# MLP's first product: raw x1 for twelve tiles, normed x1 for fifty-two, and the order of the transposes of x1

## The chip, the cores and the metric

The kernel runs on one core of a Trainium2 chip. The metric is the device time of one execution in microseconds (us); lower is better. TensorE (PE) multiplies, VectorE (DVE), ScalarE (ACT) and GpSimd (POOL) work on elements, and SyncE (SP) issues nearly all DMAs. Each engine works through its own instructions in order.

## The reference

One layer of a transformer with two recurrent branches, in float32, for 256 tokens of width D = 2048. The change touches what stands behind the branches:

```
x = x + g1 * ((gate_a * (ya @ up_a) + gate_b * (yb @ up_b)) @ out_w)      # called x1 here
h = x1 * rsqrt(mean(x1^2) + eps) * norm2_w * (1 + sc2) + sh2
x = x1 + g2 * (square(relu(h @ mlp_w1)) @ mlp_w2)                         # mlp_w1: 2048 x 8192
return rms_norm(x, final_norm_w)
```

## The kernel before

**Products in three parts.** A float32 operand is split into a high part (rounded copy in the fp32r type, on ACT) and a low part (the difference, on DVE). A product of two operands is three matmuls, high x high, high x low and low x high, added in one accumulator (`mm3`, `tokmm`).

**Weights** come in granules of 512 KB (`wgran`): SP issues the load into a `raw` buffer, then ACT copies the high part of each half of 512 columns (L235) and DVE subtracts (L236), both with the highest priority of the planner that lays out each engine's order. A pair of buffers (`hi`, `lo`) holds one half. There are three pairs (pool `stream`); from tile 6 of mix on (`RD`) four more come to them (`wide`, `NH2`), seven in all, and two more `raw` buffers to the three.

**Stages around the change.** *Mix*: 16 tiles, each one granule and 24 matmuls of 256 columns. *out_w*: four column blocks of 512; a block is eight granules of two k each (`tokmm`), 12 matmuls of 512 columns for a granule, with the weights as the moving operand; then `resid` adds the block to x (L1449, L1450: two steps on DVE for each half of the tokens). Right behind each block, its four 128-column pieces of x1 are turned by TensorE (L1477, eight transposes), scaled by norm2_w * (1 + sc2) on ACT (L1481) and split (L253, L254) into `xT[k]`, for k = 0 to 15.

*First product of the MLP* (w1), 64 tiles in two halves of 32: each tile is two granules and 16 x 3 matmuls of 258 columns. x1 is not normed: 256 columns are the scaled x1, and two more hold the shift sh2 (and a second one that is not used), so that h @ w1 comes out as rs * (x1s @ w1) + sh2 @ w1. The eviction multiplies by the row of rs (`rs_bc`, L1516), adds the shift's column inside the ReLU (L1515, L1517), squares (L1518) and splits the result into `uu[f]`. rs itself is made ahead of the first tile: `rstd` (sum on DVE, then a logarithm and an exponential on ACT, for which it loads tables, L1458, L1459), turned into a row by two matmuls (L1488). *Second product* (w2): after each half, `tokmm` over its 32 tiles, four blocks of 512 columns, 768 matmuls.

**Beside them**: `gate2` computes the gate g2 in 32 steps, each a load of 512 KB (L1410, SP) and two multiply-adds on DVE (L1416, L1418); one step stands ahead of each of the first 32 tiles in the code. The final norm's weight `fn` is loaded ahead of the first tile. Two accumulators of 512 columns alternate for `dacc`, four for `pm`. The planner lets an instruction go ahead of its place in the code when its engine would be free and its operands are there.

## Time and profile before

| | us |
|---|---|
| median of three runs | 2324.24 |
| lowest and highest of them | 2314.77 and 2326.75 |
| the profiled execution | 2329.58 |
| its span in the profile | 2327.8 |
| TensorE busy in the span | 2223.4 (96%) |
| DVE busy | 1579.1 (68%) |
| ACT busy | 1352.0 (58%) |

The profile shows one execution. "Busy" counts the time in which at least one instruction is recorded on an engine; records of matmuls overlap, as an end lies behind the next start, so the cost of a matmul in a row of them is read from start to start. Idle time in brackets is time in which nothing was recorded on the engine just ahead of the instruction, with what released it. Weight loads of TensorE have a row of their own (PEld) and lie beside the matmuls.

### The profile page before, as it was taken

The page shows a single profiled execution, that of the slowest core. Times are in us where ns is not written, and L with a number is a line of the kernel's source. Part 1 is how long each engine was busy: PE and PEld are TensorE (multiplying, and loading weights), DVE is VectorE, ACT ScalarE, POOL GpSimd, SP SyncE. Part 2 cuts the span into 40 slices and gives each one's busy share as a digit, 9 for nine tenths or more (in the row PEclk, how much of TensorE's full clock was granted, in tenths as well). Part 3 has the DMA queues.
Part 4 walks back from the last instruction along what each step waited for, and adds up shares of the span by engine and source line. Part 5 has one row for each costly group of instructions (what it writes and reads, how often), then busy time and mean ns, then how long its engine had stood idle before and what let it go on. Part 6 is the DMA issues. An engine that isn't in the chain of part 4 may idle for free.

```text
span 2327.8 us, 45179 instructions
## 1 busy us (share of the span) xinstructions
PE 2223.4 (96%) x16886; PEld 1809.3 (78%) x16886; DVE 1579.1 (68%) x3590; ACT 1352.0 (58%) x3003; POOL 159.1 (7%) x343
## 2 busy tenths in 40 slices
PE   5989999999999999999999999999999999999997
PEld 2566676767677776778888888879999888999886
DVE  2366875858686867678577766876887555666554
ACT  3244758575758575766666666555555444555543
POOL 0000021111111121111000000000000000000000
PEclk9998999999999999999999989999999999999999
DMA  9953333423333333457576455875776665555663
GB/s 369 330 177 129 103 111 106 141 89 123 109 128 116 123 118 108 138 187 245 191 228 223 159 151 162 304 256 181 258 266 217 191 194 195 182 182 182 193 195 128
DMA packets 184659, 418.20 MB, mean 180 GB/s; under 512 B 15412, under 2 KB 37364, under 8 KB 183416
## 3 DMA queue, kind: packets, MB, share of 16 engines
q1 hardware_dynamic: 183864, 414.28, 54.3%
q8 instruction: 132, 2.16, 0.4%
q10 hardware_dynamic: 576, 1.05, 0.1%
q14 instruction: 87, 0.71, 0.1%
HBM read 399.76 MB, written 15.51 MB: 178 GB/s over the span
## 4 chain that ended last, share of the span: by engine, by line
PE 73%; ACT 8%; DVE 6%; DMA 3%; issue 2%; DVEq 0%; ACTq 0%; SPq 0%
PE dacc L248 14%; PE dacc L249 13%; PE dacc L250 13%; PE dacc L1438 3%; PE dacc L1439 3%; PE dacc L1437 3%; PE pm L1437 3%; PE pm L1438 3%; PE pm L1439 3%; PE vacc L305 2%; DMA raw<-in_mod_w_dram 2%; ACT hi L235 1%; DVE lo L236 1%; PE cb L887 1%; PE pg L757 1%
## 5 line engine op out<-in xcount | busy, mean ns | idle before, releaser
L236 DVE TENSOR_TENSOR lo<-raw,hi 128x512 fp32r<-128x512 f32 (+1 forms) x1032 | 692.6, 677 | 439.0 <-ACT hi L235 264.1
L235 ACT CAST hi<-raw 128x512 fp32r<-128x512 f32 (+1 forms) x1032 | 624.5, 610 | 609.0 <-PE dacc L249 311.2
L248 PE MATMUL dacc<-hh,hi 128*128 128x256 f32 (+1 forms) x1648 | 567.1, 344 | 15.8 <-DVE sg L453 5.7
L250 PE MATMUL dacc<-hh,lo 128*128 128x256 f32 (+1 forms) x1648 | 534.6, 324 | 0.6 <-DVE lo L236 0.6
L249 PE MATMUL dacc<-hl,hi 128*128 128x256 f32 (+1 forms) x1648 | 533.7, 324 | 0.6 <-DVE hl L254 0.6
L248 PEld LDWEIGHTS dacc<-hh,hi 128*128 128x128 f32 x1648 | 317.6, 193 | 86.0 <-issue 42.6
L250 PEld LDWEIGHTS dacc<-hh,lo 128*128 128x128 f32 x1648 | 318.5, 193 | 24.4 <-issue 2.6
L249 PEld LDWEIGHTS dacc<-hl,hi 128*128 128x128 f32 x1648 | 318.9, 194 | 21.8 <-issue 3.2
L248 PE MATMUL dacc<-ah,hi 128*128 128x258 f32 x1024 | 291.9, 285 | 1.3 <-ACT ah L253 1.1
L249 PE MATMUL dacc<-al,hi 128*128 128x258 f32 x1024 | 291.1, 284 | 0.0
L250 PE MATMUL dacc<-ah,lo 128*128 128x258 f32 x1024 | 290.5, 284 | 0.0
L248 PEld LDWEIGHTS dacc<-ah,hi 128*128 128x128 f32 x1024 | 195.3, 191 | 2.8 <-ACT ah L253 1.3
L249 PEld LDWEIGHTS dacc<-al,hi 128*128 128x128 f32 x1024 | 195.1, 191 | 1.1 <-issue 1.0
L250 PEld LDWEIGHTS dacc<-ah,lo 128*128 128x128 f32 x1024 | 195.1, 191 | 0.0
L176 POOL TENSOR_SCALAR sp<-vu,pc 64x64 f32<-64x64 f32 x224 | 128.7, 574 | 432.0 <-DVE vu L176 379.8
L1438 PE MATMUL dacc<-hi,hl 128*128 128x512 f32 x320 | 125.4, 392 | 0.0
L1437 PE MATMUL dacc<-hi,hh 128*128 128x512 f32 x320 | 124.9, 390 | 0.3 <-ACT hh L253 0.3
L1439 PE MATMUL dacc<-lo,hh 128*128 128x512 f32 x320 | 125.1, 391 | 0.0
L1438 PE MATMUL pm<-hi,hl 128*128 128x512 f32 x320 | 124.8, 390 | 0.0
L1437 PE MATMUL pm<-hi,hh 128*128 128x512 f32 x320 | 124.8, 390 | 0.0
L1439 PE MATMUL pm<-lo,hh 128*128 128x512 f32 x320 | 124.7, 390 | 0.0
L494 DVE TENSOR_TENSOR ltmp<-X,Lt 128x126 f32<-128x126 f32 (+22 forms) x372 | 93.7, 252 | 8.1 <-DMA X<-in_eye_dram 0.8
(414 smaller groups left out, 3238.1 us busy)
## 6 DMA issues: line engine op xcount, KB each, us to landing
raw<-in_w_dram SPq DMA_DIRECT2D x256, 512.0 KB
raw<-in_mod_w_dram SPq DMA_DIRECT2D x96, 512.0 KB
graw<-in_mod_w_dram SPq DMA_DIRECT2D x96, 512.0 KB
raw<-in_w_gdn_dram SPq DMA_DIRECT2D x64, 512.0 KB
raw<-in_w_pg_dram SPq DMA_DIRECT2D x64, 512.0 KB
raw<-in_w_rkv_dram SPq DMA_DIRECT2D x40, 512.0 KB
raw<-in_out_w_dram SPq DMA_DIRECT2D x32, 512.0 KB
raw<-in_upa_dram SPq DMA_DIRECT2D x16, 512.0 KB
```

The lines of the kernel that those rows point to most:

```text
L176: return getattr(self.eng, name)(*a, **k)
L235: S.copy(out=hi[:, :F], in_=x)
L236: V.tensor_tensor(out=lo[:, :F], in0=x, in1=hi[:, :F].bitcast(F32), op=ALU.subtract)
L248: P.matmul(out=o, lhsT=wh, rhs=ah, start=first, stop=False)
L249: P.matmul(out=o, lhsT=wh, rhs=al, start=False, stop=False)
L250: P.matmul(out=o, lhsT=wl, rhs=ah, start=False, stop=last)
L305: P.matmul(out=pm[32 * g:32 * g + 32, :], lhsT=sc_st[:, 2 * k:2 * k + 32], rhs=raws[g // 2][:, g % 2 * 512:g % 2 * 512 + 512], start=(q == ...
L494: V.tensor_tensor(out=tv, in0=X[:, 0:n, j:j + 1].to_broadcast([128, n, 31 - j]), in1=Lt[:, j:j + 1, j + 1:32].to_broadcast([128, n, 31 - j ...
L757: P.matmul(out=q[:, c], lhsT=bkh(h, 4 + c), rhs=eb[r, h, c], start=True, stop=True)
L1437: P.matmul(out=pss[i], lhsT=ah[:, tsl], rhs=wh, start=first, stop=False)
L1438: P.matmul(out=pss[i], lhsT=al[:, tsl], rhs=wh, start=False, stop=False)
L1439: P.matmul(out=pss[i], lhsT=ah[:, tsl], rhs=wl, start=False, stop=last)
```

## The change

- The first product has two forms. The first `F0` = 12 tiles are as before. In the other 52 tiles x1 is normed and shifted already: `xN[k]` holds its high and low parts side by side, 256 columns each. One matmul of 512 columns multiplies the high weights with both, and one of 256 columns adds low weights x high part to the first half of the accumulator (`mm2`). The eviction adds the two halves, and takes ReLU and square in one step.
- `normed(k)` makes `xN[k]` from `xT[k]` during tiles 1 to 11: three steps on DVE and one on ACT for each k.
- High and low parts of an activation now lie in one tile (`hT`, `xT`, `xN`), so that one operand covers both. `xT` is four tiles `x0` to `x3`.
- Room: `xN` is new, and the four extra pairs of weight halves are gone. From tile 13 of w1 on, the space of `xT` (`x1` to `x3`) serves three more granules; of four granules three lie there and one in the `stream` pairs. `fn` goes into `x0`, loaded after the third block of the first w2 stage.
- `turned(n)`, the transposes and splits of block n, runs two granules into block n + 1 (the last one in the middle of the first tile of w1). `rstd` and its row come in the middle of the second tile, and the first tile is evicted after that. In the plain tiles the square moves from DVE to ACT.
- `gate2` steps once per two tiles from tile 12 on in the first half, then at every second granule of w2.

```diff
-NH2 = 4
-    nsplit, wide = 0, None
+    ngran, wide = 0, None
 
     def parts():
-        nonlocal nsplit
-        nsplit += 1
-        if not wide or nsplit % (3 + NH2) < 3:
-            return [stream.tile([128, 512], F32R, tag=t, name=t) for t in ("hi", "lo")]
-        return [wide.tile([128, 512], F32R, tag=t + "2", name=t, bufs=NH2) for t in ("hi", "lo")]
+        nonlocal ngran
+        ngran += 1
+        if not wide or ngran % 4 == 0:
+            return [[stream.tile([128, 512], F32R, tag=t, name=t) for t in ("hi", "lo")] for _ in range(2)]
+        w = wide.tile([128, 2, 2, 512], F32R, tag=f"x{ngran % 4}", name="w")
+        return [(w[:, i, 0, :], w[:, i, 1, :]) for i in range(2)]
         F = K // 2 * w
-        r = []
+        r = parts()
         for i in range(2):
-            hi, lo = parts()
+            hi, lo = r[i]
...
-    def mm3(o, wh, wl, ah, al, first, last):
-        P.matmul(out=o, lhsT=wh, rhs=ah, start=first, stop=False)
-        P.matmul(out=o, lhsT=wh, rhs=al, start=False, stop=False)
-        P.matmul(out=o, lhsT=wl, rhs=ah, start=False, stop=last)
-
-    def split(hi, lo, src):
-        S.copy(out=hi, in_=src)
-        V.tensor_tensor(out=lo, in0=src, in1=hi.bitcast(F32), op=ALU.subtract)
+    def mm3(o, wh, wl, a, first, last):
+
+        P.matmul(out=o, lhsT=wh, rhs=a[:, 0, :], start=first, stop=False)
+        P.matmul(out=o, lhsT=wh, rhs=a[:, 1, :], start=False, stop=False)
+        P.matmul(out=o, lhsT=wl, rhs=a[:, 0, :], start=False, stop=last)
+
+    def mm2(ps, wh, wl, a, first, last):
+
+        P.matmul(out=ps.rearrange("p (a n) -> p a n", a=2), lhsT=wh, rhs=a, start=first, stop=False, skip_group_check=True)
+        P.matmul(out=ps[:, :256], lhsT=wl, rhs=a[:, 0, :], start=False, stop=last, skip_group_check=True)
...
         for j in range(16):
             if j == RD:
-                more, wide = (big, "raw", RM, RM), big
+                more = (big, "raw", RM, RM)
...
-        def tokmm(src, kts, acts, n, done):
+        def tokmm(src, kts, acts, n, done, beside=iter(())):
 
             pss = [psum_d(), pm()]
             for i0 in range(0, len(kts), 2):
                 k0 = kts[i0]
+                if i0 % 4 == 0:
+                    next(beside, None)
                 wg = wgran(src[k0 * 128:(k0 + 2) * 128, n * 512:(n + 1) * 512].rearrange("(k p) c -> p k c", p=128))
...
-        xT = [(big.tile([128, NX], F32R, name=f"ah{k}"), big.tile([128, NX], F32R, name=f"al{k}")) for k in range(KT)]
+        xT = [t[:, k] for t in [big.tile([128, 4, 2, NX], F32R, tag=f"x{j}", name="xT") for j in range(4)] for k in range(4)]
+        xN = [big.tile([128, 2, SEQ], F32R, name=f"xN{k}") for k in range(KT)]
         sc2 = wk.tile([128, 16], F32, name="sc2", bufs=1)
         V.scalar_tensor_tensor(out=sc2, in0=modc[:, 48:64, 0], scalar=1.0, in1=W("n2", 0, 16), op0=ALU.add, op1=ALU.mult)
         for k in range(KT):
-            split(xT[k][0][:, SEQ:], xT[k][1][:, SEQ:], modc[:, 32 + k, :])
-
-        for n in range(4):
-            tokmm(A["out_w"], list(range(16)), uu[8:24], n, lambda i, n, ps: resid(i, n, ps, 0))
+            split(xT[k][:, :, SEQ:], modc[:, 32 + k, :])
+
+        def turned(n):
+
+            yield
             for k2 in range(2):
                 pt = pm()
                 for kk in range(2):
...
                     k = 4 * n + 2 * k2 + kk
                     hf = wk.tile([128, SEQ], F32, tag="hf", name="hf")
                     S.activation(out=hf, in_=pt[:, kk * 256:kk * 256 + 256], func=AF.Copy, scale=sc2[:, k:k + 1])
-                    split(xT[k][0][:, :SEQ], xT[k][1][:, :SEQ], hf)
+                    split(xT[k][:, :, :SEQ], hf)
+            yield
+
+        behind = iter(())
+        for n in range(4):
+            tokmm(A["out_w"], list(range(16)), uu[8:24], n, lambda i, n, ps: resid(i, n, ps, 0), behind)
+            behind = turned(n)
         dump("x1", xs[0])
         rs_bc = big.tile([128, SEQ], F32, name="rs_bc")
-        pt = pm()
-        rr = rstd(0)
-        for i in range(2):
-            P.matmul(out=pt[:, i * 128:(i + 1) * 128], lhsT=rr[:, i:i + 1].to_broadcast([128, 128]), rhs=ident, start=True, stop=True)
-        S.copy(out=rs_bc, in_=pt[:, :256])
 
 
         NH = 2
         FT = FF // 128 // NH
-        fn = big.tile([128, D], F32, name="fn")
-        nc.sync.dma_start(out=fn, in_=A["fnw"].to_broadcast([128, D]))
+        F0 = 12
 
         def resid2(i, n, ps):
             resid(i, n, ps, 4)
...
             if n == 0:
                 S.activation(out=ssq[i][:, 0:1], in_=ssq[i][:, 4:5], func=AF.Sqrt)
 
+        def normed(k):
+            t = wk.tile([128, SEQ], F32, tag="hf", name="t")
+            V.tensor_tensor(out=t, in0=xT[k][:, 0, :SEQ].bitcast(F32), in1=xT[k][:, 1, :SEQ].bitcast(F32), op=ALU.add)
+            V.tensor_tensor(out=t, in0=t, in1=rs_bc, op=ALU.mult)
+            sh = modc[:, 32 + k, 0:1]
+            S.activation(out=xN[k][:, 0, :], in_=t, func=AF.Identity, bias=sh)
+            V.scalar_tensor_tensor(out=xN[k][:, 1, :], in0=t, scalar=sh, in1=xN[k][:, 0, :].bitcast(F32), op0=ALU.add, op1=ALU.subtract)
+
+        def plain(f, ps):
+            rl = wk.tile([128, NX], F32, tag="rl", name="rl")
+            S.copy(out=rl[:, SEQ:], in_=ps[:, SEQ:NX])
+            V.tensor_tensor(out=rl[:, :SEQ], in0=ps[:, :SEQ], in1=rs_bc, op=ALU.mult)
+            S.activation(out=rl[:, :SEQ], in_=rl[:, :SEQ], func=AF.Relu, bias=rl[:, SEQ:SEQ + 1])
+            S.activation(out=rl[:, :SEQ], in_=rl[:, :SEQ], func=AF.Square)
+            split(uu[f], rl[:, :SEQ])
+
         g2 = gate2()
         for half in range(NH):
             for f in range(FT):
-                next(g2, None)
+                if half or f >= F0:
+                    if f == F0 + 1 and not half:
+                        wide = big
+                    if f % 2 == 0:
+                        next(g2, None)
+                    ps = psum_d()
+                    for g in range(2):
+                        wg = wgran(A["w1"][half * FT + f][:, 8 * g:8 * g + 8, :])
+                        for kk in range(8):
+                            k = 8 * g + kk
+                            mm2(ps, *wk_(wg, kk, 128), xN[k], k == 0, k == KT - 1)
+                    rl = wk.tile([128, NX], F32, tag="rl", name="rl")[:, :SEQ]
+                    S.copy(out=rl, in_=ps[:, 256:])
+                    V.tensor_tensor(out=rl, in0=ps[:, :256], in1=rl, op=ALU.add)
+                    V.scalar_tensor_tensor(out=rl, in0=rl, scalar=0.0, in1=rl, op0=ALU.max, op1=ALU.mult)
+                    split(uu[f], rl)
+                    continue
                 ps = psum_d()
                 for g in range(2):
                     wg = wgran(A["w1"][half * FT + f][:, 8 * g:8 * g + 8, :])
+                    if g == 1 and f == 0:
+                        for _ in behind:
+                            pass
+                    if g == 1 and f == 1:
+                        pt = pm()
+                        rr = rstd(0)
+                        for i in range(2):
+                            P.matmul(out=pt[:, i * 128:(i + 1) * 128], lhsT=rr[:, i:i + 1].to_broadcast([128, 128]), rhs=ident, start=True, stop=True)
+                        S.copy(out=rs_bc, in_=pt[:, :256])
+                        plain(0, ps0)
                     for kk in range(8):
                         k = 8 * g + kk
-                        mm3(ps[:, :NX], *wk_(wg, kk, 128), xT[k][0], xT[k][1], k == 0, k == KT - 1)
-                rl = wk.tile([128, NX], F32, tag="rl", name="rl")
-                S.copy(out=rl[:, SEQ:], in_=ps[:, SEQ:NX])
-                V.tensor_tensor(out=rl[:, :SEQ], in0=ps[:, :SEQ], in1=rs_bc, op=ALU.mult)
-                S.activation(out=rl[:, :SEQ], in_=rl[:, :SEQ], func=AF.Relu, bias=rl[:, SEQ:SEQ + 1])
-                V.tensor_tensor(out=rl[:, :SEQ], in0=rl[:, :SEQ], in1=rl[:, :SEQ], op=ALU.mult)
-                split(uu[f][0], uu[f][1], rl[:, :SEQ])
+                        mm3(ps[:, :NX], *wk_(wg, kk, 128), xT[k], k == 0, k == KT - 1)
+                if f == 0:
+                    ps0 = ps
+                    continue
+                for k in range((f - 1) * KT // (F0 - 1), f * KT // (F0 - 1)):
+                    normed(k)
+                plain(f, ps)
             for n in range(4):
                 tokmm(A["w2"], list(range(half * FT, (half + 1) * FT)), uu, n,
-                      resid2 if half else lambda i, n, ps: resid(i, n, ps, None))
+                      resid2 if half else lambda i, n, ps: resid(i, n, ps, None), g2)
+                if n == 2 and not half:
+                    fn = big.tile([128, D], F32, tag="x0", name="fn")
+                    nc.sync.dma_start(out=fn, in_=A["fnw"].to_broadcast([128, D]))
```

## Rows read from the trace of the kernel before

**Rows 1.** Part 4 of the page, the chain of work that ended last, the shares of the span by engine:

```profile
PE 73%; ACT 8%; DVE 6%; DMA 3%; issue 2%; DVEq 0%; ACTq 0%; SPq 0%
```

**Rows 2.** The table of stretches: from and to in us, its length, then busy us and number of instructions of PE, PEld, DVE, ACT and POOL, TensorE's granted clock as a share of full speed, the mean busy share of the DMA engines, and GB/s. The stretches are mix, out_w, the boundary to the MLP, the first w2 stage, and the second half of w1:

```profile
1441.00:1489.00 48.00, 46.07 (x371) 45.37 (x369) 42.87 (x108) 24.66 (x63) 0.00 (x0) 0.98 0.88 297
1489.00:1590.00 101.00, 97.01 (x448) 79.90 (x448) 74.34 (x128) 56.98 (x114) 0.00 (x0) 0.98 0.78 261
1590.00:1598.00 8.00, 5.81 (x41) 5.30 (x40) 3.74 (x8) 7.21 (x16) 0.00 (x0) 0.92 0.56 167
1598.00:1783.00 185.00, 184.79 (x1488) 182.33 (x1488) 145.80 (x270) 98.50 (x216) 0.00 (x0) 0.99 0.72 240
1783.00:1967.00 184.00, 184.00 (x858) 154.29 (x857) 104.12 (x157) 85.56 (x140) 0.00 (x0) 1.00 0.61 194
1967.00:2142.00 175.00, 175.00 (x1449) 174.78 (x1449) 113.82 (x212) 98.48 (x212) 0.00 (x0) 1.00 0.56 181
```

**Rows 3.** The timeline of ACT (start us, duration us, engine, line, operation and tiles), the evictions of the first and of the 32nd tile of the MLP's second half:

```profile
1962.00 0.15 ACT L1515 COPY rl<-dacc 128x2 f32<-128x2 f32 x1
...
2141.39 0.15 ACT L1515 COPY rl<-dacc 128x2 f32<-128x2 f32 x1
```

**Rows 4.** The timeline of TensorE, the first and the last of the 768 matmuls of the second w2 stage:

```profile
2140.78 0.39 PE L1437 MATMUL dacc<-hi,hh 128*128 128x512 f32 x1
...
2314.66 0.39 PE L1439 MATMUL pm<-lo,hh 128*128 128x512 f32 x1
```

**Rows 5.** The timeline of TensorE in mix, where each matmul has 256 columns: the first and the last start of a run with 69 distances, and the matmuls ahead of which it stood idle before and after it (in brackets the idle time and what ended it):

```profile
1443.27 0.28 PE L250 MATMUL dacc<-hh,lo 128*128 128x256 f32 x1
...
1451.54 0.28 PE L250 MATMUL dacc<-hh,lo 128*128 128x256 f32 x1
1452.37 0.36 PE L248 MATMUL dacc<-hh,hi 128*128 128x256 f32 x1 [0.55 <-ACT hi L235]
...
1459.05 0.38 PE L248 MATMUL dacc<-hh,hi 128*128 128x256 f32 x1 [0.69 <-DVE gt L1375]
```

**Rows 6.** The timeline of TensorE in out_w, around the two late turns of x1 (L1477):

```profile
1514.35 0.39 PE L1437 MATMUL dacc<-hi,hh 128*128 128x512 f32 x1
1516.41 0.88 PE L1477 MATMUL pm<-cs,xr 128*128 128x128 f32 x6 [1.67 <-DVE xr L1450]
...
1535.96 0.39 PE L1437 MATMUL dacc<-hi,hh 128*128 128x512 f32 x1
1538.35 0.47 PE L1477 MATMUL pm<-cs,xr 128*128 128x128 f32 x2 [2.01 <-DVE xr L1450]
...
1539.05 0.63 PE L1439 MATMUL dacc<-lo,hh 128*128 128x512 f32 x1
...
1542.04 0.41 PE L1437 MATMUL pm<-hi,hh 128*128 128x512 f32 x1
```

**Rows 7.** The timeline of TensorE at the boundary, where the first tiles of the MLP have begun:

```profile
1592.56 0.28 PE L250 MATMUL dacc<-ah,lo 128*128 128x258 f32 x1
1593.94 0.50 PE L248 MATMUL dacc<-ah,hi 128*128 128x258 f32 x2 [1.11 <-ACT ah L253]
...
1594.40 0.28 PE L250 MATMUL dacc<-ah,lo 128*128 128x258 f32 x1
1595.76 0.71 PE L1488 MATMUL pm<-cs,rstd 128*128 128x128 f32 x4 [1.08 <-ACT rstd L1459]
...
1596.67 0.42 PE L249 MATMUL dacc<-al,hi 128*128 128x258 f32 x1
...
1599.89 0.37 PE L249 MATMUL dacc<-al,hi 128*128 128x258 f32 x1
```

**Rows 8.** The timeline of ACT there, its two table loads:

```profile
1590.76 1.28 ACT L1458 ACT_TABLE_LOAD   x1
...
1594.21 1.28 ACT L1459 ACT_TABLE_LOAD   x1
```

**Rows 9.** The timelines of TensorE, ACT and DVE around the start of a granule of out_w (1505.79): the last matmul that reads the high half in question, the copies and the subtractions that follow, and the granule's first matmul:

```profile
1504.66 0.39 PE L1438 MATMUL pm<-hi,hl 128*128 128x512 f32 x1
...
1505.08 1.30 ACT L235 CAST hi<-raw 128x512 fp32r<-128x512 f32 x2 [1.42 <-PE pm L1438]
...
1505.74 1.37 DVE L236 TENSOR_TENSOR lo<-raw,hi 128x512 fp32r<-128x512 f32 x2 [1.35 <-PE pm L1438]
...
1505.79 0.39 PE L1437 MATMUL dacc<-hi,hh 128*128 128x512 f32 x1
```

**Rows 10.** The same in the first product, with 258 columns: the last matmul that reads a high half, and the copy that it releases:

```profile
2139.10 0.28 PE L249 MATMUL dacc<-al,hi 128*128 128x258 f32 x1
...
2139.42 0.62 ACT L235 CAST hi<-raw 128x512 fp32r<-128x512 f32 x1 [0.52 <-PE dacc L249]
```

**Rows 11.** Who waited for whom from 1489 to 1605 us (us in total, times, longest), the rows of DVE and the gate's weights; then the timeline of SP, the issue of the first of these loads:

```profile
DVE acc L1418 <- DMA raw<-in_mod_w_dram: 3.1, 2, 2.3
...
DVE acc L1416 <- DMA raw<-in_mod_w_dram: 2.0, 1, 2.0
...
1506.88 0.46 SPq L1410 DMA_DIRECT2D raw<-in_mod_w_dram  x1
```

**Rows 12.** The timelines of ACT and DVE in the first half of the MLP: a step of an eviction with the idle time ahead of it, and another of 256 columns:

```profile
1644.94 0.41 ACT L253 CAST hh<-rl 128x256 fp32r<-128x256 f32 x1 [2.95 <-DVE rl L1518]
...
1664.47 0.42 DVE L254 TENSOR_TENSOR hl<-rl,hh 128x256 fp32r<-128x256 f32 x1
```

34 lines of the change are left out of this document (18 added, 16 removed).

## The prediction

> **What bounds the kernel now.** I read the shares of the chain that ended last first: TensorE's steps in it are nearly three quarters of the span [rows 1]. The table by stage then says where that holds. From 1598 us on TensorE has no idle time, in the first and second product of the MLP alike; before that it is idle for 4.0 of 101 us in the stage of out_w and 2.2 of 8 us at the boundary to the MLP [rows 2]. So in the MLP only cheaper matmuls help, and ahead of it only removed waits.
>
> "Busy" does not say what a matmul costs, since their records overlap. I take the distance between starts. From the eviction of the first tile of the MLP's second half to that of its 32nd, 31 tiles of 48 matmuls take 179.39 us: 120.6 ns for each matmul of 258 columns [rows 3]. The 768 matmuls of the last w2 stage, 512 columns each, start 226.7 ns apart (173.88 us over 767 distances) [rows 4]. In mix, 69 distances of the 256-column form take 8.27 us, 119.9 ns [rows 5]. Twice the columns cost less than twice the time; that is all the first product can gain.
>
> The waits of TensorE ahead of the MLP are two and two. In out_w it starts a turn of x1 late by 2.06 and 2.39 us, both times for DVE's residual; after the second, seven distances take 2.99 us, 0.43 us each, with TensorE at the lower of its two clocks [rows 6]. At the boundary it waits 1.38 us for the high part of the last turned x1 and 1.36 us for rstd, and then runs 15 distances in 3.22 us, again at the lower clock [rows 7]. Between them ACT loads two tables of 1.28 us [rows 8].
>
> **Part by part, against the profiled execution (2329.58 us, 5.3 us above the median of the three runs shown, which itself spread from 2314.77 to 2326.75).**
>
> *Wide matmuls in 52 tiles.* Per k, three of 258 columns (3 x 120.6 = 361.7 ns) become one of 512 and one of 256 (226.7 + 119.9 = 346.6). That is 15.1 ns less, times 16 k, times 52 tiles: **-12.6 us**. All of it lies on the path, because TensorE is never idle there. The trace has no alternation of the two forms, so each is priced by its own run [rows 4, 5]. What the rows show is a cost of about 13 ns per matmul beside its columns ((226.7 - 120.6)/254 columns is 0.418 ns per column, and 120.6 less 258 of them leaves 12.8); a third of the matmuls goes, with this cost. The Trainium skill, "TensorE: Matmul & The Clock Gate", section "Back-to-back issue gap", gives a smaller fixed part, N/2.4 + 2.5 ns; by it three of 110.0 ns become 215.8 + 109.2, 5.0 ns less per k, and the term would be -4.2 us. The trace does not agree with it here: 120.6 and 226.7 ns stand against its 110.0 and 215.8.
>
> *Turning x1 amid the next tile.* The eight transposes of a column block come after two granules of the next one instead of right behind their residuals. DVE then has 5.4 us for what it was late by 1.83 and 2.16 us with (2.06 and 2.39 less one distance). Both waits go, and with them the slow stretch (2.99 - 7 x 0.227 = 1.40): **-5.4 us** [rows 6].
>
> *Scale and rstd inside the second tile.* In the code the broadcast matmul stands one and a half tiles later, 8.7 us, so its wait (1.36 - 0.12 = 1.24) goes; so should the wait of 1.26 and the slow stretch (3.22 - 15 x 0.1206 = 1.41): **-3.9 us** [rows 7]. The last block is now turned in front of k = 8 of the first tile, so k = 12 comes twelve matmuls later, 1.45 us. ACT makes two steps of 0.41 us for each k [rows 12], 3.3 us for four, and the last is needed after 1.45 + 3 x 0.36 = 2.5: a new wait of about **+0.9 us** (0 if ACT starts on the first half early, 2.9 if the lower clock comes with it), and behind it stand all further matmuls.
>
> *Three pairs of weight halves instead of seven, from tile 6 of mix to tile 12 of the MLP.* This is what the change pays with. A high part can be copied once the matmuls on the pair three back are done. In the first product ACT's copy follows the end of the last matmul that reads the pair by 0.04 us [rows 10]; copy and subtraction take about 1.4 us together, and two pairs of matmuls last 2.89 us, so some 1.7 us are to spare. In out_w the second pair of a granule is tighter: its buffer is released by the granule before, the copy starts 0.71 us ahead of the next granule and the low part is ready 0.64 us behind its start (1.37 us for two, of which the first 0.69) [rows 9], while the sixth matmul needs it at 5 x 0.227 = 1.13. Some 0.5 us are to spare. What can use them up:
> - mix: its tiles 0 to 5 had three pairs, and TensorE ran 69 distances at full pace between two stops of 0.55 and 0.69 us [rows 5]. Ten more tiles: **+1 us** (0 to 2.5).
> - out_w: the gate's loads were issued from 1506.9 us on, some 80 us ahead of the MLP in whose code they stand, and DVE, which works in order, stood still for them 2.0 us once and 3.1 us in two [rows 11]. I take it that they run ahead again, since DVE has as much room. Less 0.5 us each that leaves 3.6 us, and a little for steps of 0.7 us ahead of a low part: **+4.5 us** (0 if they no longer run ahead, 9 if the lower clock comes twice).
> - tiles 0 to 12 of the MLP: ACT stood 2.95 us behind one eviction [rows 12], 1.3 more than is to spare, and two tables are still loaded. **+2.5 us** (0 to 6).
>
> A gain is excluded for all three, because fewer buffers bring no weight earlier.
>
> *Normed x1.* Sixteen times three steps on DVE and one on ACT, beside eleven tiles (63.7 us). At 0.42 us a step [rows 12] DVE gets 20 us more, 32% on top of 65% [rows 2], less 7% for the square that moves to ACT: 90%, still covered. ACT comes to about 80%. Priced at nothing; if the cover fails, the excess of DVE over TensorE, some 2 us, is inside the last term.
>
> *Gate of the MLP and final norm's weight.* Their 32 loads and 64 steps on DVE come at every second tile from 12 on and through the first w2 stage, the weight's load in that stage's third block. There DVE was busy for 104 of 184 us and the DMA engines moved 194 GB/s [rows 2], and the weights then have 4.5 granules of buffers: nothing. SP's queue only sees them later.
>
> Sum: -12.6 - 5.4 - 3.9 + 0.9 + 1 + 4.5 + 2.5 = **-13.0 us** (-21.9 to -1.5). The profiled execution becomes 2316.6; from the median, 2324.2 - 13.0 = **2311 us**.
>
> **Rivals.**
> 1. *The buffers' price stays small.* Gate loads no longer run ahead, and 18 to 22 us come: 2302 to 2306. For it: mix with three pairs. Against it: nothing in the trace held the loads back.
> 2. *A wide matmul gains little.* Its two results lie in one accumulator, and the narrow one adds to half of it at once; if that, or loading the other half of the weights, costs as much as a matmul more, a wide one costs two of 258 columns (241.2 ns), a k becomes 361.1 instead of 361.7 ns, the term 0.5 us and the time 2323. That would also be the case of a change that does not do what it says. Against it stand the long runs at both widths, which add to one place as well [rows 3, 4]. By the Trainium skill's formula above the time would lie between, at 2320.
> 3. *Waits are traded for waits.* DVE's stops for gate loads (5.1 us in out_w) and ACT's behind evictions reach TensorE in full and with the lower clock in both stages; the terms for the buffers are 20 instead of 8: 2323.
> 4. *Slower: ACT's order.* With three pairs an ACT that waits in order for a DVE step of an eviction holds up the copy of the next pair, in tile after tile. Price: 1.3 us (2.95 less 1.7) in each of 13 tiles, 0.5 us in each of 32 granules of out_w, 0.7 us in each of ten tiles of mix, 40 us, so 2342. It decides at 21.9 us over 68 granules, 0.32 us each. Against it: mix's first six tiles have the same order of steps and lost under 2 us [rows 5].
>
> **How the numbers follow.** Forecast case, 2306 to 2316: 0.60. Rival 1: 0.10; rival 2: 0.08; rival 3: 0.14; rival 4: 0.08. Half a per cent, about what a measurement of this kernel can tell from no change, is 11.6 us, so the line lies at 2312.6; two thirds of the forecast case are below it. Faster: 0.40 + 0.10 = 0.50. Within: 0.20 + 0.08 + 0.14 = 0.42. Slower: 0.08. The range leaves out rival 4 and the best end of rival 1, and takes in rivals 2 and 3 with the spread of the runs: 2302 to 2328.
>
> **What would show it.** Tiles of the wide form should end 5.55 us apart (16 x 346.6 ns) instead of 5.79; if they end above 5.70, rival 2 holds. In out_w no wait for the residual should stand in front of a transpose. If TensorE's waits for high or low parts from tile 6 of mix to tile 12 of the MLP come to more than 15 us, rival 3 or 4 holds, told apart by whether they are stops for the gate's loads or repeat in every tile. A first wide tile that waits for normed x1, or a DVE near 100% in tiles 1 to 11, would upset the zero there.

## The result, and the profile after

The changed kernel takes 2310.62 us (median of 11 runs, 2306.71 to 2325.68), the kernel before 2326.62 beside it (11 runs, 2314.77 to 2336.95). The means, 2312.75 and 2324.79, stand at a ratio of 0.9948, 95% interval 0.9928 to 0.9968, which is 12.1 us less (7.4 to 16.8); the medians lie 16.0 apart. The forecast, 13.0 us less and 2311 us, lies inside. How it came about is mostly another story than the one forecast, and the stages show it.

The profiled execution after took 2314.76 us (span 2313.0). Its timeline of TensorE, the first matmul of mix, of out_w, of the first half of w1, its w2 stage, the second half of w1, its w2 stage, and the last matmul of all:

```profile
1431.30 0.35 PE L248 MATMUL dacc<-h,hi 128*128 128x256 f32 x1 [0.88 <-DVE gu L1285]
...
1477.46 0.40 PE L1444 MATMUL dacc<-hi,h 128*128 128x512 f32 x1
...
1575.11 0.28 PE L248 MATMUL dacc<-xT,hi 128*128 128x258 f32 x1
...
1762.56 0.39 PE L1444 MATMUL dacc<-w,h 128*128 128x512 f32 x1
...
1944.15 0.40 PE L254 MATMUL dacc<-xN,w 128*128 128x512 f32 x1
...
2123.24 0.39 PE L1444 MATMUL dacc<-w,h 128*128 128x512 f32 x1
...
2299.76 0.39 PE L1446 MATMUL pm<-lo,h 128*128 128x512 f32 x1
```

The same view of the kernel before, the five starts that the rows ahead of the prediction don't have (the last two are in [rows 4]):

```profile
1438.60 0.36 PE L248 MATMUL dacc<-hh,hi 128*128 128x256 f32 x1 [2.04 <-DVE gu L1280]
...
1489.37 0.47 PE L1437 MATMUL dacc<-hi,hh 128*128 128x512 f32 x1 [0.31 <-ACT hh L253]
...
1585.35 0.28 PE L248 MATMUL dacc<-ah,hi 128*128 128x258 f32 x1
...
1781.49 0.39 PE L1437 MATMUL dacc<-hi,hh 128*128 128x512 f32 x1
...
1955.62 0.28 PE L248 MATMUL dacc<-ah,hi 128*128 128x258 f32 x1
```

The distances of these starts are the lengths of the stages, in us, beside what the terms of the forecast come to in each (wide -4.8 and -7.7 in the two halves of w1):

| stage | before | after | difference | forecast |
|---|---|---|---|---|
| mix | 50.8 | 46.2 | -4.6 | +1 |
| out_w | 96.0 | 97.7 | +1.7 | -5.4 + 4.5 = -0.9 |
| w1, first half | 196.1 | 187.5 | -8.7 | -4.8 - 3.0 + 2.5 = -5.3 |
| w2, first | 174.1 | 181.6 | +7.5 | 0 |
| w1, second half | 185.2 | 179.1 | -6.1 | -7.7 |
| w2, second | 173.9 | 176.5 | +2.6 | 0 |
| sum | 876.1 | 868.5 | -7.6 | -13.0 |

The other 7.3 us between the two profiles lie ahead of mix (1438.60 against 1431.30), where no code differs. The kernel before profiled once more reached mix at 1430.40 us; in all 14 profiles of this study, of every version, mix began between 1423.9 and 1438.6 us, at 1432.4 on average in the five that begin as the kernel before and at 1431.3 in the nine that begin as the changed one. In the two profiles of the kernel before the stages behind it agree within 0.4 us, so they tell versions apart better than one total does. The timed 12.1 (7.4 to 16.8) just takes in 7.6: by the stages the gain is 5.4 us short of the forecast, and that the timed figure came out nearer to it is in part chance.

Part 4 of the page, the chain's shares, here adds up to 46% only, since the chain could not be followed further back; what answers to [rows 1] is that TensorE, with 38%, still has five sixths of it.

The table of stretches after, to be read beside [rows 2] (here: mix; out_w; the boundary; tiles 1 to 11; the first w2 stage. Of the six rows there the fourth, which the text ahead of them does not name, is the first half of w1 behind the boundary):

```profile
1431.00:1477.00 46.00, 45.70 (x381) 45.73 (x382) 42.26 (x110) 25.53 (x63) 0.00 (x0) 1.00 0.87 299
1477.00:1575.00 98.00, 94.57 (x414) 75.03 (x413) 71.99 (x121) 53.07 (x105) 0.00 (x0) 0.98 0.74 246
1575.00:1583.00 8.00, 7.94 (x65) 7.64 (x64) 6.47 (x14) 6.81 (x18) 0.00 (x0) 1.00 0.73 239
1583.00:1647.00 64.00, 63.23 (x524) 62.82 (x524) 52.89 (x115) 48.88 (x109) 0.00 (x0) 1.00 0.58 186
...
1762.00:1944.00 182.00, 180.53 (x779) 145.47 (x778) 112.03 (x180) 70.85 (x130) 0.00 (x0) 1.00 0.67 226
```

TensorE has 0.3 us of idle time left in mix, still 3.4 us in out_w, hardly any at the boundary, and now 1.5 us in the first w2 stage. The waits of out_w stand elsewhere than in [rows 6]. No transpose waits any more; matmuls on a granule's low or high part do (timeline of TensorE, in brackets the idle time and what ended it):

```profile
1479.09 0.50 PE L1446 MATMUL dacc<-lo,h 128*128 128x512 f32 x1 [0.30 <-DVE lo L236]
...
1481.73 0.50 PE L1444 MATMUL dacc<-hi,h 128*128 128x512 f32 x1 [0.76 <-ACT hi L235]
...
1484.39 0.67 PE L1446 MATMUL dacc<-lo,h 128*128 128x512 f32 x1 [0.97 <-DVE lo L236]
...
1506.83 0.50 PE L1446 MATMUL dacc<-lo,h 128*128 128x512 f32 x1 [0.90 <-DVE lo L236]
```

Behind the third of them the lower clock comes again: matmuls start 0.43 us apart, and the table of stretches has a granted clock of 0.50 there. SP issues the first load of the gate only then (timeline of SP):

```profile
1484.90:1487.90 3.00, 3.00 (x9) 2.32 (x8) 2.34 (x6) 1.64 (x3) 0.00 (x0) 0.50 0.92 332
```
```profile
1487.79 0.46 SPq L1415 DMA_DIRECT2D raw<-in_mod_w_dram  x1
```

So no gate load made these three waits. What made the low part of 1506.83 late is told by the chain of waits (start, us, what). A load of the gate lands after 6.49 us, VectorE stands at the gate's step until then, and the low part comes three steps behind:

```profile
1496.98 6.49 DMA raw<-in_mod_w_dram
...
1503.56 0.09 DVE acc L1423
...
1505.52 0.66 DVE acc L1423
1506.17 0.61 DVE lo L236
```

The same view of the kernel before has this ahead of its late transposes of 1516.41 [rows 6]:

```profile
1506.88 8.37 DMA raw<-in_mod_w_dram
...
1515.27 0.04 DVE acc L1416
...
1515.67 0.68 DVE xr L1450
```

For these waits it is one cause in both kernels: VectorE, which works in order, at a gate step. Only the victim differs.

At the boundary two short waits are left of those of [rows 7], without a slow stretch:

```profile
1585.81 0.71 PE L1560 MATMUL pm<-cs,rstd 128*128 128x128 f32 x4 [0.54 <-ACT rstd L1466]
...
1587.05 0.39 PE L250 MATMUL dacc<-xT,lo 128*128 128x258 f32 x1 [0.22 <-DVE lo L236]
```

Two things are new. The first tile on lent granules (tile 13) waits 2.11 us; DVE's timeline shows the eviction of tile 11 (L1525) behind a run of subtractions for the granules just come free:

```profile
1656.10 0.47 PE L254 MATMUL dacc<-xN,w 128*128 128x512 f32 x1 [2.11 <-DVE rl L1525]
```
```profile
1653.13 1.29 DVE L236 TENSOR_TENSOR w<-raw,w 128x512 fp32r<-128x512 f32 x2
1654.34 0.69 DVE L236 TENSOR_TENSOR lo<-raw,hi 128x512 fp32r<-128x512 f32 x1
1654.94 0.68 DVE L236 TENSOR_TENSOR w<-raw,w 128x512 fp32r<-128x512 f32 x1
1655.54 0.42 DVE L1525 TENSOR_TENSOR rl<-dacc,rs_bc 128x256 f32<-128x256 f32 x1
```

And in w2 not all granules take the same time. The first matmuls of the next four granules of the last stage, whose first starts at 2123.24 above:

```profile
2126.01 0.39 PE L1444 MATMUL dacc<-w,h 128*128 128x512 f32 x1
...
2128.80 0.39 PE L1444 MATMUL dacc<-w,h 128*128 128x512 f32 x1
...
2131.56 0.39 PE L1444 MATMUL dacc<-hi,h 128*128 128x512 f32 x1
...
2134.28 0.40 PE L1444 MATMUL dacc<-w,h 128*128 128x512 f32 x1
```

Twelve matmuls on the lent granules in x1, x2 and x3 ("w") take 2.77, 2.79 and 2.76 us, twelve on two pairs of the stream ("hi") 2.72, which is the 226.7 ns of [rows 4]. None of them waits. The groups of four behind these take 2.79, 2.80, 2.74 and 2.72 us: in x1 and x2 the distances are 233 ns on average, in x3 all but the first three are 226.7.

The first w2 stage has the same spacing, the gate's matmuls, and one long stop. Its chain is a weight load issued at 1870.44 us, when a subtraction between gate steps had freed the buffer, and landed 4.85 us later:

```profile
1876.58 0.50 PE L1444 MATMUL dacc<-w,h 128*128 128x512 f32 x1 [1.30 <-ACT w L235]
```

### The profile page after: what moved, and what is told of

Read it like the earlier page. It is cut to its first block, busy times and chain, and to the rows that moved or that the text cites. A ratio compares the mean times of both kernels' runs of the same rounds, so it can differ in the third digit from the quotient of the medians.

```text
span 2313.0 us, 43284 instructions
## 1 busy us (share of the span) xinstructions
PE 2207.6 (95%) x16054; PEld 1752.7 (76%) x16054; DVE 1580.5 (68%) x3626; ACT 1331.1 (58%) x2979; POOL 159.4 (7%) x343
## 5 line engine op out<-in xcount | busy, mean ns | idle before, releaser
L235 ACT CAST hi<-raw 128x512 fp32r<-128x512 f32 (+1 forms) x688 | 413.9, 604 | 518.3 <-PE dacc L249 200.4
L236 DVE TENSOR_TENSOR lo<-raw,hi 128x512 fp32r<-128x512 f32 (+1 forms) x688 | 458.4, 670 | 363.8 <-ACT hi L235 321.5
L248 PE MATMUL dacc<-h,hi 128*128 128x256 f32 (+1 forms) x1648 | 563.7, 342 | 13.1 <-DVE sg L458 5.0
L250 PE MATMUL dacc<-h,lo 128*128 128x256 f32 (+1 forms) x1648 | 531.0, 322 | 0.6 <-DVE lo L236 0.6
L249 PE MATMUL dacc<-h,hi 128*128 128x256 f32 (+1 forms) x1648 | 530.6, 322 | 0.6 <-DVE h L259 0.6
L248 PEld LDWEIGHTS dacc<-h,hi 128*128 128x128 f32 x1648 | 314.8, 191 | 81.2 <-issue 39.3
L250 PEld LDWEIGHTS dacc<-h,lo 128*128 128x128 f32 x1648 | 315.7, 192 | 24.0 <-issue 2.6
L249 PEld LDWEIGHTS dacc<-h,hi 128*128 128x128 f32 x1648 | 316.0, 192 | 21.6 <-issue 3.2
L236 DVE TENSOR_TENSOR w<-raw,w 128x512 fp32r<-128x512 f32 x344 | 219.0, 686 | 40.3 <-ACT w L235 37.9
L235 ACT CAST w<-raw 128x512 fp32r<-128x512 f32 x344 | 192.8, 617 | 60.1 <-PE pm L1446 33.2
L254 PE MATMUL dacc<-xN,w 128*128 128x512 f32 x608 | 214.2, 394 | 2.1 <-DVE rl L1525 2.1
L254 PEld LDWEIGHTS dacc<-xN,w 128*128 128x128 f32 x608 | 114.2, 188 | 29.4 <-issue 2.9
L255 PEld LDWEIGHTS dacc<-xN,w 128*128 128x128 f32 x608 | 114.0, 188 | 0.0
```

The source lines that it names most:

```text
L235: S.copy(out=hi[:, :F], in_=x)
L236: V.tensor_tensor(out=lo[:, :F], in0=x, in1=hi[:, :F].bitcast(F32), op=ALU.subtract)
L248: P.matmul(out=o, lhsT=wh, rhs=a[:, 0, :], start=first, stop=False)
L249: P.matmul(out=o, lhsT=wh, rhs=a[:, 1, :], start=False, stop=False)
L250: P.matmul(out=o, lhsT=wl, rhs=a[:, 0, :], start=False, stop=last)
L254: P.matmul(out=ps.rearrange("p (a n) -> p a n", a=2), lhsT=wh, rhs=a, start=first, stop=False, skip_group_check=True)
```

## The experiments

After the first result my theory was: from mix on the change gives some 7.5 us; wide matmuls gain less than priced, because operands lie in other places; moving the transposes removed no wait but moved it, since three pairs and VectorE's stops for gate loads remain. The rival: each term holds as forecast and the rest is the chance of one profile. Each run's stages, from the starts of the same first matmuls (us):

| run | mix | out_w | w1, first | w2, first | w1, second | w2, second | sum |
|---|---|---|---|---|---|---|---|
| before | 50.8 | 96.0 | 196.1 | 174.1 | 185.2 | 173.9 | 876.1 |
| b_again | 51.2 | 95.9 | 196.1 | 174.1 | 185.2 | 173.9 | 876.4 |
| turn_only | 51.2 | 95.4 | 194.7 | 174.1 | 185.2 | 173.9 | 874.4 |
| pairs_late | 48.3 | 96.4 | 196.0 | 177.4 | 185.2 | 177.1 | 880.3 |
| before_late | 50.1 | 90.9 | 197.7 | 174.1 | 185.2 | 173.9 | 871.8 |
| after | 46.2 | 97.7 | 187.5 | 181.6 | 179.1 | 176.5 | 868.5 |
| narrow | 46.3 | 95.3 | 189.0 | 188.3 | 183.7 | 179.9 | 882.5 |
| align | 46.2 | 97.9 | 187.1 | 181.6 | 178.3 | 173.9 | 864.9 |
| no_gate | 46.9 | 93.1 | 186.6 | 176.7 | 179.1 | 176.5 | 859.0 |
| lent | 46.1 | 97.6 | 185.9 | 181.4 | 177.9 | 173.9 | 862.8 |
| lent_gate | 47.7 | 98.4 | 192.8 | 175.0 | 177.9 | 173.9 | 865.7 |
| late_gate | 47.0 | 91.0 | 197.5 | 178.9 | 178.7 | 173.9 | 867.0 |
| late_stag | 46.1 | 90.8 | 192.8 | 178.7 | 177.9 | 173.9 | 860.3 |
| late_tied | 46.3 | 90.6 | 189.0 | 180.2 | 178.8 | 173.9 | 858.7 |

**b_again**, the kernel before, unchanged.

> The kernel before, unchanged, for a second profile. In the first pair of profiles the changed kernel reaches mix 7.3 us earlier (1431.3 against 1438.6 us), in code that the change leaves as it was but for where activations lie. If that is chance of one execution: this profile reaches mix at another time than 1438.6, anywhere from 1430 to 1440, and its stages from mix on keep their lengths to within 1 us (mix 50.8, out_w 96.0, w1 196.1 and 185.2, first w2 174.1). If the layout of the activations made the early part faster: 1438.6 to within 1 us.

2321.70 us. The stages agree within 0.4 us, the way to mix does not (8.2 us). So the 7.3 us ahead of mix are no more than chance brings about.

**turn_only**, the kernel before with the transposes amid the next tile and rstd inside the second tile, nothing else:

```diff
-        for n in range(4):
-            tokmm(A["out_w"], ..., lambda i, n, ps: resid(i, n, ps, 0))
-            (eight transposes, scaling, split)
+        for n in range(4):
+            tokmm(A["out_w"], ..., lambda i, n, ps: resid(i, n, ps, 0), behind)
+            behind = turned(n)
```

> The kernel before with one part of the change alone: transposes two granules into the next block, rstd and its row in the middle of the second tile; seven pairs, the gate's steps and the narrow product stay. By the forecast's steps: no wait for a residual in front of a transpose, out_w from 96.0 to about 90.6 us, the boundary about 3 us shorter, in all -8.4 us (ratio 0.9964). Rival: the waits come back elsewhere, because DVE still stops for the gate's loads while it has the residuals to do; then out_w stays above 94 us and the ratio is within 0.002 of 1.

2319.26 us, ratio 0.9991 (0.9965 to 1.0017); out_w 0.6 us shorter, w1's first half 1.4. At the boundary one distance of 0.81 us, for rstd, is left, as in the changed kernel (0.82); distances of 1.79 and 0.94 us for evictions (at 1655.38 and 1697.75 us) take back much of that gain. With seven pairs out_w's wait stays in front of a transpose, only a later one and longer:

```profile
1539.25 1.75 PE L1479 MATMUL pm<-cs,xr 128*128 128x128 f32 x7 [3.78 <-DVE xr L1452]
```

**narrow**, the changed kernel with three matmuls of 256 columns in the normed tiles:

```diff
-                            mm2(ps, *wk_(wg, kk, 128), xN[k], k == 0, k == KT - 1)
+                            mm3(ps[:, :256], *wk_(wg, kk, 128), xN[k], k == 0, k == KT - 1)
```

> The changed kernel with the normed product in three matmuls of 256 columns instead of one of 512 and one of 256, and the eviction without the addition of the two halves. By the forecast's step a k takes 3 x 119.9 = 359.7 instead of 350 ns: second half of w1 +5.0 us, the twenty tiles of the first +3.1, in all +8 us against the changed kernel, ratio to before about 0.998. Rival, that a wide matmul gains little: less than 3 us between the two.

2323.15 us, ratio 1.0000 (0.9975 to 1.0026). The second half of w1 is 4.6 us longer than after (183.7 against 179.1; 512 k, so 9.0 ns per k): the wide form gains. Both w2 stages are longer too (6.7 and 3.4 us). Their matmuls are spaced as in after, so all of it is in stops; why the narrow form leads to them stays open.

**align**, the changed kernel with every lent granule on the same place in 256 bytes as the stream's pairs. The tiles x1 to x3 hold 4 x 2 x 258 x 4 = 8256 bytes, 64 more than a multiple of 256, so each starts 64 further (xN, behind them, moves too):

```diff
+        big.tile([128, 48], F32, name="pad")
-        big.tile([128, 4, 2, NX], F32R, tag=f"x{j}", name="xT")
+        big.tile([128, 2112], F32R, tag=f"x{j}", name="xT")   (its first 8 * NX used)
```

> The changed kernel with 192 bytes of padding ahead of the tiles x0 to x3 and these 8448 instead of 8256 bytes long, so that granules in x1 to x3 and normed x1 begin at the same place within 256 bytes as the weights in the stream pairs. In the changed kernel's w2, matmuls on granules in x1 and x2 start 233 ns apart, in x3 and in the stream pairs 226.7. Theory of placement: all at 226.7, second w2 stage 2.7 us shorter, the wide form at 346 to 347 ns per k instead of 350; first half of w1 -1, second half -1.8, each w2 -2.7: about -8 us against the changed kernel, ratio to before about 0.991. Rival, that PE's reads meet ACT's and DVE's writes into the neighbouring part of the same granule: nothing changes, 233 ns stays.

2311.94 us, ratio 0.9946 (0.9925 to 0.9967). The second w2 stage is back at 173.9 (-2.6), the second half of w1 at 178.3 (348.2 ns per k instead of 349.8). The first w2 stage stays at 181.6: its wide spacing falls from 2.6 to 0.2 us, and its stops grow from 2.3 to 4.8, with three distances of 1.12, 1.28 and 1.81 us for weights. By the sum of the stages 3.6 of the 8 us expected have come. The placing costs what it seemed to: x3, which stands three steps of 64 bytes behind x0, is already where the pad of 192 bytes puts them all, and its matmuls were already at 226.7 ns. The first w2 stage is bound by something else.

**pairs_late**, the kernel before with its four extra pairs from out_w on only:

```diff
-                more, wide = (big, "raw", RM, RM), big
+                more = (big, "raw", RM, RM)
             mix(j)
+        wide = big
```

> The kernel before, with its four extra pairs of big used only from out_w on; the mix product has the three pairs of stream, as in the changed kernel. Theory A (the four extra pairs let the copies and subtractions of out_w's granules run ahead of mix's own evictions on ScalarE and VectorE, and that made mix's stops of 0.7 to 1.5 us): mix falls from 51 us to 46 to 47 us and the rest stays within 1 us of the kernel before (out_w 95 to 97 us). Theory B (mix is shorter for another reason, such as the joined layout of hT): mix stays at 50 to 51 us.

One execution, 2323.64 us. Mix takes 48.3 us, between the two theories. It has no stop left inside, and one at its end, where out_w's first granule stands behind it:

```profile
1476.74 0.47 PE L1438 MATMUL dacc<-hi,hh 128*128 128x512 f32 x1 [1.89 <-DVE gt L1375]
```

Without that (2.17 us from the matmul ahead, less 0.12) it is 46.2, the length after: the extra pairs made mix's stops, ahead of tiles 4, 6 and 9 and at its end. How, VectorE's timeline in the kernel before shows for the stop of 1459.05 [rows 5]: the eviction that it waits for (L1375) stands behind subtractions for later granules:

```profile
1457.03 1.29 DVE L236 TENSOR_TENSOR lo<-raw,hi 128x512 fp32r<-128x512 f32 x2
...
1458.58 0.41 DVE L1375 SCALAR_TENSOR_TENSOR gt<-gt,dacc 128x256 f32<-128x256 f32 x1
```

Unasked for, the shift also put these pairs on another place in 256 bytes (64 further, by the sizes of the tiles now made ahead of them), and both w2 stages grew by 3.2 us or more, without a stop: the placing again, in the other kernel.

**no_gate**, the changed kernel without the second gate's loads, steps and matmuls:

```diff
-        g2 = gate2()
+        g2 = iter(())
```

> The changed kernel without the second gate (its 32 loads, its VectorE steps and its four matmul pairs are left out, and the first gate is used again in its place). Theory A (the gate's loads hold up out_w's weight granules, and its matmul pairs of about 1.3 us each lie in the first w2 stage): out_w falls from 97.7 to 93 to 94 us, the first w2 stage from 181.6 to 177 us (2.8 us of which is the wider spacing of the matmuls on x1 and x2), the first half of w1 by 1 to 3 us. Theory B (three pairs starve out_w by themselves, and w2's stops come from its own loads): out_w stays at 97 to 98 us and the first w2 stage above 179 us.

One execution, 2303.47 us: out_w 4.6 us shorter, the first w2 stage 4.9, the first half of w1 0.9. Theory A has these sizes, but not all of the 4.6 can be put down to the loads: 2.0 of it, most of that the lower clock, lie in the first three granules (the fourth starts 10.95 us into the stage here, 12.99 in the changed kernel), whose waits come ahead of the changed kernel's first gate load. The other 2.6 come behind it. What is left in out_w with three pairs are the stops of its first 7 us; what is left in the first w2 stage (176.7) is the second one's length, so nothing but the place.

**lent**, align with the space of xN8 to xN15 as four more pairs until tile 4 of w1:

```diff
+            if npair % 7 < 3:  r.append([stream.tile(...) for t in ("hi", "lo")])
+            else:              r.append([lent.tile(..., tag=f"xN{...}") for t in ("hi", "lo")])
```

> The aligned version of the changed kernel, with the space of xN8 to xN15 lent as four extra pairs of the stream from out_w to the fourth tile of w1, seven in all as in the kernel before. Theory A (three pairs are what out_w lost): out_w 92 to 93 us instead of 97.9, the rest as in the aligned version, total about 5 us below it, 2307 us. Theory B (the loads that come late are the cause, and buffers change nothing): out_w stays at 96 to 98 us, total 2312 us.

2306.83 us, ratio 0.9937 (0.9908 to 0.9965); out_w is not shorter (97.6), though the total came out as theory A has it. The stops for low parts are gone, and the waits ahead of the transposes are back (timeline of TensorE, then the chain of waits):

```profile
1515.45 1.75 PE L1498 MATMUL pm<-cs,xr 128*128 128x128 f32 x7 [2.40 <-DVE xr L1466]
...
1541.70 0.98 PE L1498 MATMUL pm<-cs,xr 128*128 128x128 f32 x7 [1.84 <-DVE xr L1466]
```
```profile
1501.30 6.85 DMA raw<-in_mod_w_dram
...
1509.18 0.74 DVE acc L1432
...
1514.79 0.61 DVE xr L1466
```

So theory B held for out_w: the buffers decide who waits. That the gate's loads set its length the runs below show, 90.6 to 91.0 us without them.

**lent_gate**, lent with the gate asked for earlier (eight steps at tile 0, then one a tile):

```diff
-                    if f % 2 == 0:
-                        next(g2, None)
+                    next(g2, None)
+                if f == 0:
+                    for _ in range(8):
+                        next(g2)
```

> As lent, with the second gate's first eight steps asked for at the start of w1 (the planner is free to draw them into out_w), then one step a tile from tile 12 on, so that fewer of its matmul pairs lie in the first w2 stage. Theory A (the gate's matmul pairs and loads lengthened that stage, and its work beside tiles 12 and 13 the stop ahead of tile 13): the first w2 stage falls from 181.6 to about 177 us, the first half of w1 grows by the matmul pairs that come back to it, at most 2 us; total 3 us below lent. Theory B (the pairs only move, and loads drawn into out_w hold up its granules): out_w grows by as much as the w2 stage loses, total within 2 us of lent.

2310.45 us, ratio 0.9946 (0.9924 to 0.9968). The first w2 stage fell by 6.4 us, the first half of w1 rose by 6.9, where theory A had 2 at most, and out_w, where theory B had the loss, by 0.8. The longest distances in w1 are 2.63 us in the second tile and 2.81 ahead of tile 13, with the lower clock behind each. The chain of the first names ScalarE with the two table loads of rstd ahead of the copies of the last turned x1, and no gate step; that the steps drawn in brought this order about is not shown. Moved, not saved.

**before_late**, the kernel before with the gate's loads held back until rs_bc is there:

```diff
         S.copy(out=rs_bc, in_=pt[:, :256])
+        for _ in range(2):
+            d = wk.tile([128, 1024], F32, tag="raw", name="raw", bufs=2)
+            V.tensor_scalar(out=d[:, :2], in0=rs_bc[:, :2], scalar1=0.5, ...)
```

> The kernel before, with the second gate's loads held back by two tiny VectorE writes into their buffers that need rs_bc, so that none can be issued during out_w. Theory A (in out_w VectorE stands in its own order at gate steps whose loads have not landed, the residual sums behind them come late, and so the transposes wait 2.06 and 2.39 us): both waits and the slow stretch behind the second go, out_w falls from 96 to 90 to 91 us; the first half of w1 grows by at most 2 us. Theory B (the transposes wait for the products' own eviction and sums, 1.4 us and more at each block whatever else VectorE does): out_w stays at 94 us or more.

2315.84 us, ratio 0.9982 (0.9961 to 1.0003). Out_w is 5.1 us shorter, with the transposes where they always were; the first half of w1 is 1.6 longer. The table of that stretch (TensorE busy for all but 0.27 us, at the full clock), and the longest of DVE's waits in it (us in total, times, longest), with no gate step among them:

```profile
1480.60:1571.50 90.90, 90.63 (x409) 74.22 (x410) 61.41 (x104) 52.64 (x105) 0.00 (x0) 1.00 0.67 221
```
```profile
DVE lo L236 <- PE pm L1438: 19.5, 17, 1.3
DVE lo L236 <- ACT hi L235: 7.8, 10, 2.6
```

**late_gate**, lent with the gate held back until tile 11, a step a tile from tile 12, the last twelve in the first w2 stage:

```diff
+                if f == F0 - 1:   (two writes as above, from xN[15])
-                    if f % 2 == 0:
-                        next(g2, None)
+                    next(g2, None)
```

> As lent (aligned, seven pairs in out_w), with the second gate's loads held back until the last normed tile, one step a tile from tile 12 on, and the last twelve steps at every eighth k tile of the first w2 stage. Theory A (the gate's place cost out_w 4 to 7 us and the first w2 stage's late loads another 4): out_w 90 to 91 us instead of 97.6, the first half of w1 186 to 190, the first w2 stage 175 to 176 instead of 181.4; from mix on 865 to 868 us instead of 875.8, time about 2299 us. Theory B (what leaves out_w comes back in tiles 12 to 31, where VectorE has about 1.8 us a tile free): the first half of w1 193 us or more, time within 3 us of lent, 2305 us.

2308.84 us, ratio 0.9954 (0.9939 to 0.9970). Out_w is 91.0 as theory A has it, but the first half of w1 is 197.5, beyond theory B's 193: a distance of 3.52 us ahead of tile 13, with a granted clock of 0.50 behind it (1658.20 to 1662.60 us), 1.39 and less later. The first w2 stage (178.9) misses theory A's 175 to 176.

**late_stag**, late_gate with the lent granules taken into use one by one:

```diff
-        if not wide or ngran % 4 == 0:
+        if not wide or not 0 < ngran % 4 <= upto:      (upto 1, 2, 3 at tiles 13, 14, 15)
```

> As late_gate, with the three lent granules of x1 to x3 taken into use one at tile 13, two at 14, three at 15, instead of all at tile 13. Theory A (the stop of 1.7 to 2.8 us ahead of tile 13 comes from the copies and subtractions of three granules at once, ahead of the eviction of tile 11 in VectorE's order): the stop falls below 0.8 us and the first half of w1 is 1.5 to 2.5 us shorter than in late_gate. Theory B (the stop is a weight load that came late): it stays above 1.5 us.

2311.56 us, ratio 0.9949 (0.9933 to 0.9965). The stop ahead of tile 13 is gone, the first half of w1 4.7 us shorter: it was the run of copies and subtractions for several granules at once, with some 2 us of the lower clock behind it. The largest distance left in the first w2 stage, 2.38 us, has this chain:

```profile
1829.36 6.81 DMA raw<-in_mod_w_dram
...
1836.27 0.06 DVE acc L1432
...
1836.93 0.69 DVE w L245
```

**late_tied**, late_stag with each gate step's coefficients taken through the low part of the granule ahead of it, so that steps can't bunch:

```diff
+                    V.scalar_tensor_tensor(out=sc, in0=tie[:, :4].bitcast(F32), scalar=0.0,
+                                           in1=sc_st[:, 4 * q:4 * q + 4], op0=ALU.mult, op1=ALU.add)
-                            V.scalar_tensor_tensor(out=acc, in0=x, scalar=sc_st[:, 2 * k:2 * k + 1], ...)
+                            V.scalar_tensor_tensor(out=acc, in0=x, scalar=sc[:, 2 * r:2 * r + 1], ...)
```

> As late_stag, with every gate step after the second granule of its tile and its two coefficients copied (times 0 and added) from the low part of that granule, so that VectorE's order can't bring the steps together: one a tile in w1, one every eighth k tile in the first w2 stage. Theory A (the stops left there, 2.32 us in w1 and 2.38 us in w2, are VectorE standing at a gate step whose load was issued 6.8 us before, the granule's low part behind it): they go, the first half of w1 188 to 191 us instead of 192.8, the first w2 stage 175.5 to 176.5 instead of 178.7, from mix on 868 to 870 us. Theory B (the stops are the weight loads queued behind gate loads on SP, or the DMA engines' own limit): stops of over 1 us stay in both, from mix on 873 us or more.

2304.66 us, ratio 0.9921 (0.9892 to 0.9949), the best of all here. The first half of w1 went to 189.0 as theory A has it. The first w2 stage did not (180.2): a stop of over 1 us stays there, as theory B has it. Its largest distance, 1.37 us, no longer has a gate load in its chain but a weight load, issued when a subtraction had freed its buffer, behind a gate step. From mix to the end it takes 871.5 us, between the two theories. The sum of the stages is 17.4 us below that of before, and the timed ratio means 18.3 us less than 2322.29:

```profile
1806.93 5.72 DMA raw<-in_w_dram
...
1812.75 0.63 ACT hi L245
```

## Why the forecast was right, and where it was not

The timed total was right, and in part by luck: by the stages the gain is 7.6 us instead of 13.0. Of the forecast's steps three were wrong, the wide matmuls were priced too high and the three pairs in out_w too low, and the place of the lent granules was not priced; in part these made up for each other. By the prediction's steps:

*Wide matmuls, -12.6.* Right in kind, too large in size. The second half of w1 took 361.6 ns per k before and 349.8 after (185.2 and 179.1 us over 512), 11.8 less instead of 15.1; over 52 tiles -9.8 us. About half of the missing 3.2 ns per k is the place of the operands in 256 bytes: 348.2 in align, 347.5 in lent, against 346.6 by the two runs in one form. Tiles are 5.60 us apart, so rival 2 falls. The Trainium skill's "TensorE: Matmul & The Clock Gate", section "Back-to-back issue gap", by whose formula the term was -4.2 (it calls that the gap of an isolated matmul, and has other figures for a stream with weight loads between), is not borne out by these rows.

*Turning x1 amid the next tile, -5.4.* This step failed. I read the wait ahead of the transposes as one for their residual, which a later place removes, and priced the gate's stops as another wait that fewer buffers might let through. The chain shows that they are the same stops: no wait is left in front of a transpose, as forecast, but the stops stand elsewhere. Moving the transposes alone gives 0.6 us in out_w (turn_only); holding back the gate's loads and moving nothing gives 5.1 (before_late).

*Three pairs, out_w, +4.5.* The stops that I named came, so the sum of the stage was only 2.6 us off, but the term was too small. Seven pairs without gate loads take 90.8 or 90.9 us (late_stag, before_late). Before, 5.1 came to that for the gate. After, it is 2.6 for the gate, 2.3 for three pairs instead of seven (93.1 in no_gate against 90.8 in late_stag), and 2.0 in the first three granules that no_gate does not have and that no gate load can have made; why they are there stays open. This is rival 3's trade, in one stage; TensorE's idle time for high and low parts up to tile 12, 3.7 us, stays far below the 15 from which that rival or the fourth would have held.

*Three pairs, mix, +1.* Wrong in sign: -4.6. "A gain is excluded for all three, because fewer buffers bring no weight earlier" overlooked that a pair that is free lets the next granule's copy and subtraction, which have priority, run ahead of mix's own eviction on ACT and DVE, and TensorE waits for that. pairs_late shows it. The run of [rows 5] lies in tiles 1 to 3, and both stops shown there come behind it, not one on either side; with three pairs alone neither is there. Of the 4.6 us 1.5 are something else: in the profile before, the first tile of mix ran at the lower clock (granted 0.50 from 1440 to 1443 us), behind a wait of 2.04 us ahead of mix.

*Scale and rstd, -3.9 + 0.9.* Borne out: of the waits of 1.11 and 1.08 us idle and the slow stretch of 1.41 [rows 7], 0.54 and 0.22 are left and no slow stretch, some 2.8 us less.

*Tiles 0 to 12, +2.5.* Near in size, but another thing: the plain tiles hardly lost anything, and 2.11 us of idle time went ahead of tile 13 to the granules that all come free at once (late_stag takes that stop away).

*Normed x1, 0.* Held: DVE was busy for 53 of 64 us in tiles 1 to 11, 83% where I had 90%.

*Gate moved, 0.* This failed as well: w2's first stage grew by 7.5 us. From start to start, 2.6 of it are the wider spacing, which no_gate keeps. The other 4.9 are the gate's (no_gate): 2.6 for three of its four pairs of matmuls (0.87 us each), which lay in w1 before, and 2.3 for late weights. I went by DVE's and the DMA engines' shares there, and counted neither the matmuls nor that a gate step ahead of a subtraction delays the buffer for a load that needs 5.72 us (late_tied). The 2.6 us that moved with the matmuls come back in w1, which fell by 8.7 instead of 5.3.

*Not priced at all:* the place of the lent granules, 2.6 us in each w2 stage, which align takes out of the second.

What stays open: the stops of the first w2 stage that only weight loads explain (late_tied), the longer w2 stages of narrow, the longer first waits of out_w, and what sets the time to mix.

## What to carry to other kernels

Before you price a wait by the instruction that ended it, follow the chain one step further, to what that engine was standing at: here both forms of the wait, 5.1 us in one kernel and 2.6 in the other, hung on loads of a later stage that were issued early and on VectorE's order. Buffers for weights that are free early are no pure gain where the copies into them have priority over evictions. Where a tile's space is lent to operands of matmuls, keep the place in 256 bytes that the other operands have.

## What the runs showed of the hardware

Matmuls of 512 columns on granules in x1 and x2, which by the sizes of the tiles stand 128 and 64 bytes from x3's place in 256, start about 233 ns apart instead of the 226.7 in x3, in the stream and in align, without any idle time (2.79 and 2.80 us against 2.72 for twelve); the length of the last w2 stage followed the place (173.9 us before and in align, 176.5 after, 177.1 in pairs_late). A load of 512 KB issued amid the stream of weights landed after 4.85 to 8.37 us in the chains above. TensorE was at the lower clock behind a wait of 0.97 us in out_w (1484.39), where 0.30 and 0.76 us of waits had come shortly before. Behind the wait of 2.11 us ahead of tile 13 it was not (granted clock 1.00 from 1656.20 to 1660.00 us); behind one of 2.21 us at the same place in lent_gate it was (0.50 from 1655.20 to 1657.90). The time to mix scattered by 13.9 us over nine profiles with the same code ahead of it; the stages behind agreed within 0.4 in the two profiles of one kernel.
